# Attention of a hybrid encoder block: TensorE's order written out for all eight query blocks

## Chip, core and metric

The kernel runs on one core of a Trainium2 chip. The metric is the device time of one execution in microseconds, the median of three runs of the same program. TensorE's clock is 1.2 or 2.4 GHz, as granted; the profile gives it as a share of 2.4.

## What is computed

One layer on 1024 tokens of width 1024 in float32: a half-step feed-forward network (SwiGLU) with a layer norm, a mixer with a layer norm, and a second feed-forward network with a layer norm. Half of the mixer's width is a gated linear attention, the other half a sparse attention of 8 heads of width 64. Only the second matters here. For each query an indexer scores all admissible keys, and the best 256 are kept; then each head computes

```python
_, idx = lax.top_k(score, topk)
...
logits = jnp.einsum('bqhd,bqkhd->bqhk', qb, kg).astype(jnp.float32) * scale
logits = jnp.where(valid[:, :, None, :], logits, -jnp.inf)
p = jax.nn.softmax(logits, axis=-1)
return jnp.einsum('bqhk,bqkhd->bqhd', p.astype(vg.dtype), vg)
```

and the two halves, side by side, are multiplied by the output weights.

## The kernel before

The kernel gathers no keys. A mask of 0 and -1e30 per query and key (`bias`, which lies in the tiles of the scores) takes the place of the selection, and all keys up to the query block's end are used. The queries come in 8 blocks of 128 (b = 0 to 7); block b sees n = 128 (b + 1) keys. `attend_block` (L1043) does one block, in four pairs q of heads h = 2q + j:

- **Logits** (L1063, L1064): queries are the stationary operand, 128 x 128, keys the moving one, in chunks of 256 to 512 columns. Query and key are split into a high and a low part (`qq`, `ql`, and the key tiles named `xh` for even and `xl` for odd heads), so each chunk takes two matmuls into the PSUM tile `lg`, two of which exist.
- **Reduction** (L1067): VectorE adds the mask, writes `e` and the row's maximum `mx`; `nm` (L1078) is the scaled negative maximum. ScalarE makes the exponentials in place and their sum `sm` (L1079). Three `e` tiles take turns.
- **Transposes** (L1087): TensorE turns `e` in pieces of 128 x 128, up to four pieces to a PSUM tile `tpe` (a group); VectorE copies the even head's group to an SBUF tile `et` (L1092), ScalarE the odd head's (L1090). Blocks 4 to 7 have two groups a head. There are four `et` tiles. The PSUM tiles `tpe`, `rb` and `tp` share two banks.
- **Value products** (L1099): per block of keys and head, the values (128 keys x 64) are stationary, the transposed numerators the moving 128 columns. The even head writes partitions 0 to 63 of the PSUM tile `pv`, the odd head 64 to 127; so they use the array as 128 x 64 (`128*64` in the profile), while logits and transposes use it as 128 x 128.
- **End of a block**: VectorE copies `pv` to the right half of the tile `cat` (L1103); eight more 64-wide matmuls spread the reciprocals of the sums over `rb` (L1109), and VectorE multiplies (L1112).

Around it, `run` (L1452) loads the left half of `cat` by DMA, and for the first half of the tokens splits `cat` into high and low parts for the output projection (`split_cat`: transposes `tp` at L184), projects the previous block (`proj_tok`: `pt`, L654 to L656, 24 matmuls of 512 columns), adds to x1 and stores. `load_q` (L1030) brings the queries of the next block in four transfers, issued by SP.

No order is written out here. The program is built under a scheduler (`TileContext(nc, schedule_with_timeline_sim=True)`, L1578) that keeps data dependencies and buffer reuse, and otherwise orders each engine's instructions by its own estimate of times. `in_order` (L143) is the means against it: it chains all TensorE instructions made inside it in the order of the code. Before, it is used in the feed-forward parts only. Each engine executes its list strictly in order.

Of the kernel before, what the change touches and what calls it, by code (L numbers as in the profile page):

```python
# [18 lines left out]
P = 128  # L19
# [96 lines left out]
class Block:  # L116
    def __init__(self, ctx, tc, aps):
# [17 lines left out]
        self._ntile = 0  # L135
        self.fill = []
# [6 lines left out]
    def in_order(self, *engines):  # L143
# [7 lines left out]
        for i in body[start:]:  # L151
            if i.engine in (engines or (mybir.EngineType.PE,)):
# [7 lines left out]
                prev[i.engine] = i  # L160

# [881 lines left out]
    def attend_block(self, b, kst, vt, bias, q_dram, qp, ep, tp, rp, ps, cat):  # L1043
        nc = self.nc
        V = nc.vector
        n = (b + 1) * P
        w = n if n <= 512 else n // 2
        nch = n // w
        qq, ql = self.q_tiles[b]
        if b + 1 < NB and b + 1 not in self.q_tiles:  # L1050
            self.load_q(b + 1, q_dram, qp[(b + 1) % 2])
        po = self.ps_pj.tile([P, 4, P], F32, tag="pj", name=self.uid("pv"))
        sm = tp.tile([P, 8], F32, tag="sm", name=self.uid("sm"), bufs=2)
        for q in range(4):
            es = []
            for j in range(2):
                h = 2 * q + j
                k = kst[j][:, q, :]
                pl = ps.tile([P, 2, 512], F32, tag="lg", name=self.uid("lg"), bufs=2)
                for c in range(nch):  # L1060
                    out = pl[:, c, : max(w, 256)]
                    ks = slice(c * w, c * w + max(w, 256))
                    nc.tensor.matmul(out, qq[:, h, :], k[:, ks], start=True, stop=False)  # L1063
                    nc.tensor.matmul(out, ql[:, j, q, :], k[:, ks], start=False, stop=True)  # L1064
                e = ep[(2 * q + j) % 3].tile([P, T], F32, tag="e", name=self.uid("e"), bufs=1)
                mx = self.small.tile([P, 1], F32, tag="mx", name=self.uid("mx"))
                V.tensor_tensor_reduce(  # L1067
                    out=e[:, :n].rearrange("p (c w) -> p c w", c=nch),
                    in0=pl[:, :nch, :w],
                    in1=bias[b].rearrange("p (c w) -> p c w", c=nch),  # L1070
                    scale=1.0,
                    scalar=NEG,
                    op0=ALU.add,
                    op1=ALU.max,
                    accum_out=mx,
                )
                nm = self.small.tile([P, 1], F32, tag="nm", name=self.uid("nm"))
                V.tensor_scalar(nm, mx, -0.125, None, ALU.mult)  # L1078
                nc.scalar.activation(e[:, :n], e[:, :n], AF.Exp, bias=nm, scale=0.125, accum_out=sm[:, h : h + 1])  # L1079
                es.append(e)  # L1080
            for g in range(0, b + 1, 4):
                m = min(4, b + 1 - g)
                ets = []
                for j in range(2):
                    pt = self.ps_tp.tile([P, 4, P], F32, tag="tp", name=self.uid("tpe"))
                    for i in range(m):
                        nc.tensor.transpose(pt[:, i, :], es[j][:, (g + i) * P : (g + i + 1) * P], self.ident)  # L1087
                    et = tp.tile([P, 4, P], F32, tag="et", name=self.uid("et"), bufs=4)
                    if j:
                        nc.scalar.activation(et[:, :m, :], pt[:, :m, :], AF.Copy)  # L1090
                    else:
                        V.tensor_copy(et[:, :m, :], pt[:, :m, :])  # L1092
                    ets.append(et)
                for i in range(m):
                    kb = g + i
                    for j in range(2):
                        h = 2 * q + j
# [484 lines left out]
```

## Times and profile before

| what | value |
|---|---|
| median of 3 runs | 2049.46 us (2046.78 to 2050.31) |
| the profiled execution | 2050.26 us, its span 2048.5 us |
| TensorE matmuls | 1997.3 us busy (98%), mean granted clock 0.981 |
| VectorE, ScalarE, GpSimd | 72%, 40%, 28% busy |
| attention, first logits to last copy of `pv` | 1132.69 to 1314.10 us of the span |

Busy TensorE time is the union of records whose modelled ends overlap the next record, so a busy stretch can still hold slack: starts have to be compared with starts. A value product or a sum (the 64-wide work) leaves two records in the trace, every other matmul of the attention one.

### The profile page before, as it was taken

What the parts mean: (1) busy time and instruction counts of PE and PEld (TensorE: products, weight loads), DVE (VectorE), ACT (ScalarE), POOL (GpSimd) and SP (SyncE); (2) the same over time, 40 slices, a digit from 0 to 9 for tenths busy, and PEclk for the clock granted to TensorE, in tenths of its full rate; (3) what the DMA queues carried; (4) which work ended last, traced back from release to release, by engine and by line L of the source; (5) the groups of instructions that cost most, each with busy time, mean ns of one, the idle gap of its engine ahead of it and who ended that gap; (6) DMA issues with size and microseconds to landing.
All of it is one profiled execution on the core that took longest, in us unless ns stands there. A gap on an engine that the chain in (4) does not pass through costs nothing.

```text
span 2048.5 us, 26941 instructions
## 1 busy us (share of the span) xinstructions
PE 1997.3 (98%) x9752; PEld 1623.9 (79%) x9752; DVE 1474.6 (72%) x2326; ACT 824.5 (40%) x1320; POOL 581.1 (28%) x497
## 2 busy tenths in 40 slices
PE   8999999999999999998998999999999999999997
PEld 6888888888888788777876677787888888888886
DVE  5588788785668768899965455567687777766577
ACT  4332322324334445888253444334323323334341
POOL 3345444440001112144152000035354454420001
PEclk9999999999999999998997799999999999999999
DMA  5345445369656222022156430242354454487664
GB/s 174 114 144 186 144 154 185 134 230 322 195 177 205 89 93 83 11 63 73 32 140 160 121 80 17 89 169 73 124 183 147 143 181 154 146 279 272 201 194 150
DMA packets 192709, 298.44 MB, mean 146 GB/s; under 512 B 16304, under 2 KB 98368, under 8 KB 192576
## 3 DMA queue, kind: packets, MB, share of 16 engines
q1 hardware_dynamic: 192576, 296.72, 44.6%
q8 instruction: 77, 1.26, 0.2%
q14 instruction: 56, 0.46, 0.1%
HBM read 205.96 MB, written 90.70 MB: 145 GB/s over the span
## 4 chain that ended last, share of the span: by engine, by line
PE 87%; DVE 5%; ACT 3%; DMA 2%; issue 1%; POOL 1%; SPq 0%; POOLq 0%; DVEq 0%; ACTq 0%
PE pd L481 19%; PE pq L310 14%; PE pq L311 14%; PE pq L309 14%; PE pf L641 3%; PE pf L642 3%; PE pf L643 3%; PE pv L1099 3%; PE pt L654 2%; PE pt L655 2%; PE pt L656 2%; PE tpe L1087 2%; DVE junk L767 1%; PE tp L255 1%; PE lg L1063 1%
## 5 line engine op out<-in xcount | busy, mean ns | idle before, releaser
L97 DVE TENSOR_TENSOR wloq<-rw,whiq 128x512 fp32r<-128x512 f32 (+1 forms) x208 | 211.9, 1021 | 111.4 <-ACT whiq L96 110.8
L97 DVE TENSOR_TENSOR wlod<-rd,whid 128x1024 fp32r<-128x1024 f32 x154 | 186.2, 1219 | 130.4 <-ACT whid L96 129.6
L96 ACT ACTIVATE whid<-rd 128x1024 fp32r<-128x1024 f32 x154 | 160.9, 1059 | 244.7 <-PE pd L481 173.1
L96 ACT ACTIVATE whiq<-rw 128x512 fp32r<-128x512 f32 (+1 forms) x208 | 163.5, 806 | 224.1 <-POOL rw L295 94.2
L481 PE MATMUL pd<-wlod,whid 128*128 128x512 f32 x616 | 239.7, 389 | 0.8 <-DVE wlod L97 0.8
L481 PE MATMUL pd<-whid,wlod 128*128 128x512 f32 x616 | 239.3, 389 | 0.0
L481 PE MATMUL pd<-whid 128*128 128x512 f32 x616 | 234.9, 391 | 0.7 <-ACT whid L96 0.7
L309 PE MATMUL pq<-b_h,whiq 128*128 128x512 f32 x576 | 228.9, 398 | 2.2 <-ACT b_h L96 2.2
L310 PE MATMUL pq<-b_l,whiq 128*128 128x512 f32 x576 | 225.4, 391 | 0.9 <-DVE b_l L97 0.9
L311 PE MATMUL pq<-b_h,wloq 128*128 128x512 f32 x576 | 225.1, 391 | 0.0
L197 POOL TENSOR_TENSOR rs<-ve,neghalf 128x1 f32<-128x1 f32 x24 | 33.8, 1410 | 630.5 <-DVE ve L215 630.5
L421 ACT ACTIVATE c<-c 128x512 f32<-128x512 f32 x80 | 50.4, 632 | 238.2 <-DVE c L345 146.6
L309 PE MATMUL pq<-xh,whiq 128*128 128x512 f32 x352 | 137.7, 391 | 0.0
L311 PE MATMUL pq<-xh,wloq 128*128 128x512 f32 x352 | 137.0, 389 | 0.0
L310 PE MATMUL pq<-xl,whiq 128*128 128x512 f32 x352 | 136.9, 389 | 0.0
L481 PEld LDWEIGHTS pd<-wlod,whid 128*128 128x128 f32 x616 | 115.6, 188 | 25.4 <-DVE wlod L97 1.6
L481 PEld LDWEIGHTS pd<-whid 128*128 128x128 f32 x616 | 115.6, 188 | 25.0 <-ACT whid L96 1.3
L481 PEld LDWEIGHTS pd<-whid,wlod 128*128 128x128 f32 x616 | 115.6, 188 | 24.0
L654 PE MATMUL pt<-whi,xh 128*128 128x512 f32 x320 | 128.3, 402 | 5.3 <-ACT stage L1397 3.3
L309 PEld LDWEIGHTS pq<-b_h,whiq 128*128 128x128 f32 x576 | 108.7, 189 | 23.9 <-ACT b_h L96 2.8
L655 PE MATMUL pt<-wlo,xh 128*128 128x512 f32 x320 | 127.0, 398 | 0.1
L311 PEld LDWEIGHTS pq<-b_h,wloq 128*128 128x128 f32 x576 | 108.7, 189 | 23.2
(253 smaller groups left out, 4538.5 us busy)
## 6 DMA issues: line engine op xcount, KB each, us to landing
rw<-in_ffn_w_gu_dram SPq DMA_DIRECT2D x88, 512.0 KB, 4.2
rd<-h_dram SPq DMA_DIRECT2D x154, 256.0 KB, 3.4
h_dram<-c SPq DMA_DIRECT2D x148, 256.0 KB, 3.0
rt<-in_ffn_w_down_dram SPq DMA_DIRECT2D x44, 512.0 KB, 3.4
t_dram<-rt SPq DMA_DIRECT2D x44, 512.0 KB, 2.9
rd<-t_dram SPq DMA_DIRECT2D x88, 256.0 KB, 4.0
rd<-in_ffn_w_down_dram SPq DMA_DIRECT2D x66, 256.0 KB, 4.0
raw<-in_w_in_dram SPq DMA_DIRECT2D x20, 512.0 KB, 4.0
```

Source lines behind the costliest of these rows:

```text
L96: self.nc.scalar.activation(hi, src, AF.Copy)
L97: self.nc.vector.tensor_sub(lo, src, hi)
L309: mm(bank, wh[:, k, :], xh[:, k, :], start=(start and k == 0), stop=False)
L310: mm(bank, wh[:, k, :], xl[:, k, :], start=False, stop=False)
L311: mm(bank, wl[:, k, :], xh[:, k, :], start=False, stop=(stop and k == 3))
L481: nc.tensor.matmul(bank, left, right, start=(i == 0 and n == 0), stop=(i == ng - 1 and n == 2))
L641: nc.tensor.matmul(pt[:m], wh[:, k, :m], xh[:, k, :], start=(k == 0), stop=False)
L642: nc.tensor.matmul(pt[:m], wh[:, k, :m], xl[:, k, :], start=False, stop=False)
L643: nc.tensor.matmul(pt[:m], wl[:, k, :m], xh[:, k, :], start=False, stop=(k == KD - 1))
L654: nc.tensor.matmul(pt, xh[:, k, cols], wh[:, k % 2, :], start=(k == 0), stop=False)
L655: nc.tensor.matmul(pt, xh[:, k, cols], wl[:, k % 2, :], start=False, stop=False)
L1099: nc.tensor.matmul(po[j * 64 : j * 64 + 64, q, :], v, ets[j][:, i, :], start=(kb == 0), stop=(kb == b))
```

## The change

The loop over blocks and pairs becomes one sequence over all 64 heads, numbered x = 8b + h, and 32 pairs p. `attend` takes the place of `attend_block`, with `begin(b)` and `end(b)` for what `run` did around it. Four inner functions hold the old steps: `logits(x)`, `turned(x)` (transposes and copies), `values(p)` (the value products of both heads of a pair over all their blocks of keys, heads alternating) and `divided(b)`. TensorE's order is chained by `in_order`: three heads' logits first, then per pair the transposes of the even head, the logits of head 2p + 3, the transposes of the odd head, the logits of head 2p + 4, and the products. The work of `end` is made inside `any_order`, which leaves it out of the chain, so the scheduler still places it. Two details change with it: `e` tiles turn by x instead of the head's number in the block, and the engine that copies a group alternates by head and group, not by head alone.

```diff
@@ in_order @@
-            if i.engine in (engines or (mybir.EngineType.PE,)):
+            if i.engine in (engines or (mybir.EngineType.PE,)) and i.name not in self.loose:
+    @contextmanager
+    def any_order(self):
+        last = self.nc.cur_bb.bb.instructions[-1]
+        yield
+        body = self.nc.cur_bb.bb.instructions
+        start = next(k for k in reversed(range(len(body))) if body[k] is last) + 1
+        self.loose.update(i.name for i in body[start:])
@@ attend_block, now attend @@
-    def attend_block(self, b, kst, vt, bias, q_dram, qp, ep, tp, rp, ps, cat):
+    def attend(self, kst, vt, bias, q_dram, qp, ep, tp, rp, ps, begin, end):
-        for q in range(4):
-            es = []
-            for j in range(2):
-                h = 2 * q + j
...
-                e = ep[(2 * q + j) % 3].tile([P, T], F32, tag="e", name=self.uid("e"), bufs=1)
...
-            for g in range(0, b + 1, 4):
-                m = min(4, b + 1 - g)
-                ets = []
-                for j in range(2):
-                    pt = self.ps_tp.tile([P, 4, P], F32, tag="tp", name=self.uid("tpe"))
-                    for i in range(m):
-                        nc.tensor.transpose(pt[:, i, :], es[j][:, (g + i) * P : (g + i + 1) * P], self.ident)
...
-                    if j:
-                        nc.scalar.activation(et[:, :m, :], pt[:, :m, :], AF.Copy)
-                    else:
-                        V.tensor_copy(et[:, :m, :], pt[:, :m, :])
-                    ets.append(et)
-                for i in range(m):
-                    kb = g + i
-                    for j in range(2):
...
+        def logits(x):
+            b, h = divmod(x, 8)
...
+            e = ep[x % 3].tile([P, T], F32, tag="e", name=self.uid("e"), bufs=1)
...
+        def turned(x):
...
+            for g in range(0, b + 1, 4):
...
+                if (x + g // 4) % 2:
+                    nc.scalar.activation(et[:, :m, :], pt[:, :m, :], AF.Copy)
+                else:
+                    V.tensor_copy(et[:, :m, :], pt[:, :m, :])
+                ets[x].append(et)
+        def values(p):
...
+            et = [ets.pop(2 * p + j) for j in range(2)]
+            for kb in range(b + 1):
                 for j in range(2):
+                    h = 2 * q + j
+                    nc.tensor.matmul(
+                        out[b][j * 64 : j * 64 + 64, q, :],
+                        vt[kb // 4][:, kb % 4, h * 64 : (h + 1) * 64],
+                        et[j][kb // 4][:, kb % 4, :],
+                        start=(kb == 0),
+                        stop=(kb == b),
+                    )
+        def divided(b, cat):
...
+        with self.in_order():
+            for x in range(3):
+                logits(x)
+            for p in range(4 * NB):
+                b, q = divmod(p, 4)
+                if q == 0:
+                    cat = begin(b)
+                    if b + 1 < NB and b + 1 not in self.q_tiles:
+                        self.load_q(b + 1, q_dram, qp[(b + 1) % 2])
+                turned(2 * p)
+                logits(2 * p + 3)
+                turned(2 * p + 1)
+                logits(2 * p + 4)
+                values(p)
+                if q == 3:
+                    divided(b, cat)
+                    with self.any_order():
+                        end(b, cat)
@@ run @@
-                for b in range(NB):
+                def begin(b):
...
-                    self.attend_block(b, kst, vt, bias, q_dram, qp, ep, tp, rp, ps, c)
+                    return c
+                def end(b, c):
                     if b < 4:
                         self.split_cat(c, b, [[c0[0]], [c0[1]]])
...
+                self.attend(kst, vt, bias, q_dram, qp, ep, tp, rp, ps, begin, end)
```

Outside the attention both programs list the same instructions in the same order on all engines. Inside, TensorE's lists read as follows; line numbers of the changed program differ: L1075 and L1076 are the logits, L1102 the transposes, L1118 the products, L1134 the sums, L1512 and L1510 the store and load of x1's half, L1047 and L1048 those of the queries.

TensorE at the last pair of block 4, before (the stretch that rows 3 show):

```order
L1087 MATMUL tpe_10579<-ident,e_10562 128x128 x4
L1099 MATMUL pv_10393<-et_10553,vt_9597 64x128
L1063 MATMUL lg_10671<-xl_9579,qq_9588 128x384
L1064 MATMUL lg_10671<-xl_9579,ql_9589 128x384
L1063 MATMUL lg_10671<-xl_9579,qq_9588 128x384
L1064 MATMUL lg_10671<-xl_9579,ql_9589 128x384
L1087 MATMUL tpe_10586<-ident,e_10573 128x128 x4
L1099 MATMUL pv_10393<-et_10584,vt_9596 64x128
L1087 MATMUL tpe_10601<-ident,e_10562 128x128
L1099 MATMUL pv_10393<-et_10591,vt_9596 64x128
L1099 MATMUL pv_10393<-et_10584,vt_9596 64x128
L1099 MATMUL pv_10393<-et_10591,vt_9596 64x128
```

and the same pair in the change, from the transposes of its odd head on:

```order
L1102 MATMUL tpe_10613<-ident,e_10552 128x128 x4
L1102 MATMUL tpe_10620<-ident,e_10552 128x128
L1075 MATMUL lg_10624<-xh_9578,qq_9588 128x384
L1076 MATMUL lg_10624<-xh_9578,ql_9589 128x384
L1075 MATMUL lg_10624<-xh_9578,qq_9588 128x384
L1076 MATMUL lg_10624<-xh_9578,ql_9589 128x384
L1118 MATMUL pv_10471<-et_10596,vt_9596 64x128
L1118 MATMUL pv_10471<-et_10618,vt_9596 64x128
L1118 MATMUL pv_10471<-et_10596,vt_9596 64x128
L1118 MATMUL pv_10471<-et_10618,vt_9596 64x128
L1118 MATMUL pv_10471<-et_10596,vt_9596 64x128
L1118 MATMUL pv_10471<-et_10618,vt_9596 64x128
```

A first product no longer stands alone between transposes: both heads' transposes and the next logits come first, and ten products follow each other, of which six are shown.

TensorE at the end of block 6, before (`pv` of one number is block 6, `rb` its sums):

```order
L1099 MATMUL pv_10911<-et_11147,vt_9597 64x128
L1109 MATMUL rb_11164<-ident,rc_11162 64x128 x8
L1063 MATMUL lg_11244<-xh_9578,qq_9588 128x512
L1064 MATMUL lg_11244<-xh_9578,ql_9589 128x512
L1063 MATMUL lg_11244<-xh_9578,qq_9588 128x512
L1064 MATMUL lg_11244<-xh_9578,ql_9589 128x512
L1099 MATMUL pv_10911<-et_11153,vt_9597 64x128
L1099 MATMUL pv_10911<-et_11147,vt_9597 64x128
L1099 MATMUL pv_10911<-et_11153,vt_9597 64x128
L1099 MATMUL pv_10911<-et_11147,vt_9597 64x128
L1099 MATMUL pv_10911<-et_11153,vt_9597 64x128
L1063 MATMUL lg_11255<-xl_9579,qq_9588 128x512
```

and in the change:

```order
L1118 MATMUL pv_10993<-et_11144,vt_9597 64x128
L1118 MATMUL pv_10993<-et_11168,vt_9597 64x128
L1134 MATMUL rb_11198<-ident,rc_11196 64x128 x8
L1102 MATMUL tpe_11210<-ident,e_11113 128x128 x4
L1102 MATMUL tpe_11217<-ident,e_11113 128x128 x4
L1075 MATMUL lg_11224<-xl_9579,qq_9588 128x512
L1076 MATMUL lg_11224<-xl_9579,ql_9589 128x512
L1075 MATMUL lg_11224<-xl_9579,qq_9588 128x512
L1076 MATMUL lg_11224<-xl_9579,ql_9589 128x512
L1102 MATMUL tpe_11235<-ident,e_11151 128x128 x4
L1102 MATMUL tpe_11242<-ident,e_11151 128x128 x4
L1075 MATMUL lg_11249<-xh_9578,qq_9588 128x512
```

Where the next logits and the rest of the products followed the sums, the transposes of the next block's first head now follow them, and logits only after these.

SP's queue in blocks 1 and 2, before (`x_dram<-score` is the store of x1's half, `score<-x_dram` the next load, `qq` and `ql` the queries of block 3):

```order
L1455 DMA cat_10387<-og_dram 128x512
L1038 DMA ql_9589<-q_lo_82 64x4x128
L1037 DMA qq_9588<-q_hi_81 64x8x128 x2
L1467 DMA x_dram<-score_6535 128x512
L1038 DMA ql_9589<-q_lo_82 64x4x128
L1464 DMA score_6535<-x_dram 128x512
L1455 DMA cat_10652<-og_dram 128x512
```

and in the change:

```order
L1499 DMA cat_10421<-og_dram 128x512
L1048 DMA ql_9589<-q_lo_82 64x4x128
L1047 DMA qq_9588<-q_hi_81 64x8x128
L1513 DMA x_dram<-score_6535 128x512
L1047 DMA qq_9588<-q_hi_81 64x8x128
L1048 DMA ql_9589<-q_lo_82 64x4x128
L1510 DMA score_6535<-x_dram 128x512
L1499 DMA cat_10686<-og_dram 128x512
```

The store of x1 has moved ahead of the second half of a query load.

## Rows read from the trace of the kernel before

**Rows 1.** The page of the profiled execution: the span, part 1 (busy time of each engine, share of the span, instructions) and part 4 (the chain that ended last, by engine).

```profile
span 2048.5 us, 26941 instructions
...
PE 1997.3 (98%) x9752; PEld 1623.9 (79%) x9752; DVE 1474.6 (72%) x2326; ACT 824.5 (40%) x1320; POOL 581.1 (28%) x497
...
PE 87%; DVE 5%; ACT 3%; DMA 2%; issue 1%; POOL 1%; SPq 0%; POOLq 0%; DVEq 0%; ACTq 0%
```

**Rows 2.** Busy time by stretches, one row for each query block 0 to 7. The first stretch begins with the first logits, each ends where the copy L1103 of its block starts. Columns: length, then busy us and instructions of TensorE, its weight loads, VectorE, ScalarE and GpSimd, the granted TensorE clock as a share of 2.4 GHz, the busy share of the DMA engines, GB/s.

```profile
1132.69:1148.61 15.92, 15.29 (x64) 10.39 (x64) 7.03 (x43) 7.29 (x32) 2.04 (x3) 0.53 0.70 186
1148.61:1166.10 17.49, 16.40 (x109) 11.89 (x110) 9.26 (x37) 7.57 (x23) 0.00 (x0) 1.00 0.59 136
1166.10:1185.59 19.49, 19.07 (x133) 13.95 (x134) 10.54 (x33) 8.30 (x22) 0.00 (x0) 1.00 0.33 83
1185.59:1208.16 22.57, 22.25 (x167) 17.25 (x168) 12.77 (x36) 10.33 (x23) 0.00 (x0) 1.00 0.29 82
1208.16:1236.77 28.61, 27.59 (x197) 20.48 (x198) 14.73 (x38) 11.54 (x26) 0.00 (x0) 1.00 0.18 47
1236.77:1261.20 24.43, 24.12 (x191) 17.43 (x192) 14.11 (x34) 11.88 (x24) 0.00 (x0) 1.00 0.16 34
1261.20:1288.47 27.27, 26.38 (x217) 19.33 (x216) 15.73 (x36) 13.00 (x23) 0.00 (x0) 1.00 0.00 1
1288.47:1314.10 25.63, 24.23 (x229) 18.56 (x228) 14.94 (x32) 13.66 (x25) 0.00 (x0) 1.00 0.06 16
```

**Rows 3.** Timeline of TensorE alone at the end of block 4. Columns: start (us), time from the first start to the last modelled end, line, operation, output<-inputs, tile of the array, shape, records merged (a value product leaves two records, a transpose or a logits matmul one).

```profile
1228.05 1.09 PE L1099 MATMUL pv<-et,vt 128*64 128x128 f32 x16
1229.08 0.66 PE L1087 MATMUL tpe<-ident,e 128*128 128x128 f32 x4
1229.66 0.43 PE L1099 MATMUL pv<-et,vt 128*64 128x128 f32 x2
...
1230.83 0.60 PE L1087 MATMUL tpe<-ident,e 128*128 128x128 f32 x4
1231.36 0.43 PE L1099 MATMUL pv<-et,vt 128*64 128x128 f32 x2
1231.72 0.33 PE L1087 MATMUL tpe<-ident,e 128*128 128x128 f32 x1
1232.18 1.09 PE L1099 MATMUL pv<-et,vt 128*64 128x128 f32 x14
1233.19 0.33 PE L1087 MATMUL tpe<-ident,e 128*128 128x128 f32 x1
```

**Rows 4.** Timeline of SP's DMA issues, from block 0 to the start of block 2 (columns as above; the time is that of issuing).

```profile
1139.64 0.63 SPq L1038 DMA_DIRECT2D ql<-q_lo  x1
...
1141.02 0.92 SPq L1455 DMA_DIRECT2D cat<-og_dram  x2
...
1157.81 0.58 SPq L1038 DMA_DIRECT2D ql<-q_lo  x1
...
1162.29 0.57 SPq L1038 DMA_DIRECT2D ql<-q_lo  x1
```

**Rows 5.** DMA issues with their time to landing, issues between 1139.5 and 1140.2 us. Columns: output<-input, queue, count, size, median us from issue to landing.

```profile
ql<-q_lo SPq DMA_DIRECT2D x1, 128.0 KB, 4.8
```

**Rows 6.** The same view, issues between 1141.0 and 1141.5 us.

```profile
cat<-og_dram SPq DMA_DIRECT2D x1, 256.0 KB, 7.7
```

**Rows 7.** Timeline of TensorE alone around the first logits of block 1 and the end of block 0.

```profile
1143.35 0.69 PE L1099 MATMUL pv<-et,vt 128*64 128x128 f32 x2
1143.97 0.58 PE L1063 MATMUL lg<-xh,qq 128*128 128x256 f32 x1
...
1149.08 0.60 PE L184 MATMUL tp<-ident,cat 128*128 128x128 f32 x4
```

**Rows 8.** Timeline of VectorE alone at the end of block 5.

```profile
1261.20 0.69 DVE L1103 COPY cat<-pv 128x512 f32<-128x512 f32 x1
1261.81 0.14 DVE L1078 TENSOR_SCALAR nm<-mx 128x1 f32<-128x1 f32 x1
...
1262.83 0.68 DVE L1112 TENSOR_TENSOR cat<-cat,rb 128x512 f32<-128x512 f32 x1
```

**Rows 9.** Groups of instructions of the whole attention (1132.6 to 1316 us), shapes kept apart. Columns: line, engine, operation, output<-inputs, shapes, count | busy us, mean ns of one | idle time of the engine just before, and what ended it.

```profile
L1099 PE MATMUL pv<-et,vt 128*64 128x128 f32 x576 | 61.9, 287 | 2.2 <-ACT et L1090 1.5 <-DVE et L1092 0.4
...
L1099 PEld LDWEIGHTS pv<-et,vt 128*64 128x64 f32 x576 | 39.4, 138 | 22.0 <-issue 10.3 <-ACT et L1090 4.4 <-ACT e L1079 2.5
...
L1067 DVE CUSTOM_DVE_ANT_0 e<-lg,score 128x1024 f32<-128x1024 f32 x8 | 9.6, 1218 | 1.2 <-PE lg L1064 0.9 <-PE tpe L1087 0.3
...
L1078 DVE TENSOR_SCALAR nm<-mx 128x1 f32<-128x1 f32 x64 | 9.3, 150 | 0.9
L1079 ACT ACTIVATE e<-e,nm 128x1024 f32<-128x1024 f32 x8 | 9.1, 1144 | 3.2 <-DVE nm L1078 3.2
```

**Rows 10.** What TensorE's matmuls waited for in the attention (1132 to 1316 us): who waited <- for whom: us in total, times, longest.

```profile
PE tpe L1087 <- DVE et L1092: 2.0, 4, 0.8
PE pv L1099 <- ACT et L1090: 1.5, 4, 0.4
PE tpe L1087 <- DVE cat L1112: 1.1, 3, 0.5
```

More of the change, by code (lines that the diff above doesn't have):

```diff
@@ L135, in __init__ @@
         self._ntile = 0
+        self.loose = set()
         self.fill = []
@@ L1081, in attend_block @@
+        def turned(x):
+            b = x // 8
+            e = es.pop(x)
+            ets[x] = []
             for g in range(0, b + 1, 4):
                 m = min(4, b + 1 - g)
[L1083 to L1093 removed]
@@ L1094, in attend_block @@
-                for i in range(m):
-                    kb = g + i
-                    for j in range(2):
-                        h = 2 * q + j
-                        v = vt[kb // 4][:, kb % 4, h * 64 : (h + 1) * 64]
-                        nc.tensor.matmul(
-                            po[j * 64 : j * 64 + 64, q, :], v, ets[j][:, i, :], start=(kb == 0), stop=(kb == b)
-                        )
-        dsa = cat[:, 512:].rearrange("p (k t) -> p k t", k=4)
-        V.tensor_copy(dsa, po)
@@ L1104, in attend_block @@
-        rc = rp.tile([P, 8], F32, tag="rc", name=self.uid("rc"), bufs=2)
-        V.reciprocal(rc, sm)
-        rb = self.ps_tp.tile([P, 4, P], F32, tag="tp", name=self.uid("rb"))
-        for h in range(8):
-            rows = slice(h % 2 * 64, h % 2 * 64 + 64)
-            nc.tensor.matmul(
-                rb[rows, h // 2, :], rc[:, h : h + 1].to_broadcast([P, 64]), self.ident, start=True, stop=True
-            )
-        V.tensor_mul(dsa, dsa, rb)
+                pt = self.ps_tp.tile([P, 4, P], F32, tag="tp", name=self.uid("tpe"))
@@ new lines, in turned @@
+                for i in range(m):
+                    nc.tensor.transpose(pt[:, i, :], e[:, (g + i) * P : (g + i + 1) * P], self.ident)
+                et = tp.tile([P, 4, P], F32, tag="et", name=self.uid("et"), bufs=4)
+                if (x + g // 4) % 2:
[6 more added lines that the diff above has]
+            if q == 0:
+                out[b] = self.ps_pj.tile([P, 4, P], F32, tag="pj", name=self.uid("pv"))
+            et = [ets.pop(2 * p + j) for j in range(2)]
+            for kb in range(b + 1):
+                for j in range(2):
+                    h = 2 * q + j
[5 more added lines that the diff above has]
+                        stop=(kb == b),
+                    )
@@ new lines, in divided @@
+        def divided(b, cat):
+            dsa = cat[:, 512:].rearrange("p (k t) -> p k t", k=4)
+            V.tensor_copy(dsa, out.pop(b))
+            rc = rp.tile([P, 8], F32, tag="rc", name=self.uid("rc"), bufs=2)
+            V.reciprocal(rc, sums.pop(b))
+            rb = self.ps_tp.tile([P, 4, P], F32, tag="tp", name=self.uid("rb"))
+            for h in range(8):
+                rows = slice(h % 2 * 64, h % 2 * 64 + 64)
+                nc.tensor.matmul(
+                    rb[rows, h // 2, :], rc[:, h : h + 1].to_broadcast([P, 64]), self.ident, start=True, stop=True
+                )
+            V.tensor_mul(dsa, dsa, rb)
```

63 lines of the change are left out of this document (33 added, 30 removed).

## Prediction

> **What bounds the kernel now.** I read the page first: over the program TensorE is busy 98% of the span, and the chain that ended last lies on it for 87% [rows 1]. So a change pays by what TensorE's own sequence loses, not by what another engine saves. Both programs list the same instructions in the same order on every engine outside the attention, so I then cut the trace at the eight copies L1103 that end the query blocks. In each block TensorE is busy all but 0.3 to 1.4 us, VectorE only 44 to 58% of the time [rows 2]. Blocks 1 to 7 run at 2.4 GHz; block 0 runs almost wholly at 1.2 GHz (mean grant 0.53), while the DMA engines are 0.70 busy.
>
> "Busy" hides the loss, because each record (0.29 us for half a value product [rows 9]) overlaps its neighbours. So I read from start to start, on TensorE's timeline [rows 3]. A value product takes 1231.72 - 1231.36 = **0.36 us** alone, between transposes; in a run, eight take 1229.08 - 1228.05 = **1.03 us** and seven take 1233.19 - 1232.18 = 1.01 us. In a run the products of a pair's two heads overlap two by two, and the place of a missing partner is paid for. Alone a product fills two places, so a place costs (1.02 - 0.36) / 6 = 0.11 us, and each run pays 0.14 us once. The neighbours pay too. A transpose streams 128 columns as half a product does; at 0.11 us each, four need 0.44. Up to a product, four that follow logits take 1231.36 - 1230.83 = 0.53 us, four that also follow a product 1229.66 - 1229.08 = 0.58 us. So the turn to products costs 0.09 to 0.12, the turn back 0.05. Together a run of 64-wide work (products and the sums rb, L1109) costs **0.31 us, and 0.11 us for each place** (its instructions, rounded up to an even number).
>
> **The change, part by part.**
>
> *Products in one run.* Counted in the two orders, from the first logits to the end of the attention: 89 runs now, 82 of odd length, 434 places for 352 instructions; in the change 37 runs, 10 odd, 362 places. The order shows why: now a pair's first product stands alone, then come a transpose and the others. Saved are 52 x 0.31 + 72 x 0.11 = 16.1 + 7.9 = **24.0 us**; by block, 0 to 7: 1.6, 1.1, 1.6, 1.6, 4.4, 5.5, 4.9, 3.4. The late blocks, with two groups of keys, have the most runs now.
>
> *Block 0 gives nothing.* SP's queue does not move there. The last transfer of block 1's queries is issued at 1139.64 [rows 4] and lands 4.8 us later [rows 5], at 1144.4. The first logits of block 1, which start at 1143.97 now [rows 7], are pinned in the change ahead of block 0's last two pairs of products: three lone products at 1143.97 - 1143.35 = 0.6 us each and a transpose less lie before them, so TensorE is there at about 1142 and waits some 2.4 us, with everything behind it. The first `cat` is issued at 1141.02 [rows 4] and lands 7.7 us later [rows 6], at 1148.7; the transposes that read it (1149.08 now, [rows 7]) follow block 0, as before. So block 0 still ends near 1148.6, and I strike out its 1.6: **-22.4 us**.
>
> *The end of a block.* In the change the sums and then the next block's transposes follow at once, where now logits lie between. The second PSUM tile of transposes after the sums needs their bank, free after VectorE's copy and multiplication: from the last product 0.3 us to its end, 0.61 to the next start on VectorE, 0.68, and two handovers of 0.05 [rows 8], 1.7 us. TensorE has 0.9 us of sums and 0.44 of transposes to do meanwhile; 0.4 is left, taken as 0.5, at seven boundaries: **+3.5 us**. Bounds: 0, and 1.7 each or 12 us, if a reduction of 1.22 us [rows 9] is in VectorE's way every time. I take the low value because VectorE is idle over 40% of each of these blocks [rows 2].
>
> *Waits that go.* TensorE waits 2.0 + 1.5 us for copies of transposed numerators now and 1.1 us for that bank [rows 10]. With the next logits between the last transposes and the products, I let 3.5 of these 4.6 go; bounds 0 and 4.6. The two terms cancel: **0**, bounds -4.6 and +12.
>
> *Logits ahead.* Between a head's logits and its transposes now lie two other heads' logits, a run of products and a transpose group; in block 7, with 16 places, over 4 us. Reduction, scaling and exponential need 1.22 + 0.15 + 1.14 = 2.5 us [rows 9]. Nothing is late. That `e` tiles turn by the running number makes each three heads old also over a block's end; hidden by the same margin, nothing.
>
> *At nothing.* The copies of groups alternate otherwise, but stay 48 on ScalarE and 48 on VectorE. On SP a store of x1 moves ahead of half a query load in three blocks; the load has a whole block (17 us or more) until its logits, and its issues take 1157.81 to 1162.29 now [rows 4]. If that cover were gone, see rival 3.
>
> Sum: 2050.26 - 22.4 = 2027.9 us for the profiled execution. The median of the three runs is 0.8 lower: the forecast is **2027 us**.
>
> One rule of the Trainium skill speaks against the largest term: "TensorE: Matmul & The Clock Gate", under "The mechanism" in Part 3, lets weight loads run beside matmuls only where their row groups differ, and both heads' products use all rows. By that rule it would be rival 4, 2034. The rows disagree: eight products hold 16 loads of 138 ns [rows 9], 2.2 us, within their 1.03 us [rows 3].
>
> **Rivals.**
> 1. *Copies become the bound.* If at half of the 28 pairs of blocks 1 to 7 the products wait 1 us for a copy behind a reduction on VectorE, that is +14: 2041. For it: VectorE works in order, with reductions of up to 1.22 us [rows 9]. Against: it has 14.9 us to do in a block 7 that shrinks from 25.6 to 22.2 [rows 2]. By the skill's "TensorEngine Tiling (Array Packing)", PSUM Bottleneck, packing products leaves the copies out of PSUM as they were and may make them the bound; these busy shares say not yet.
> 2. *The clock stays low.* The wait of 2.4 us lies in the stretch at 1.2 GHz. Were block 1 at 1.2 GHz too, its 16.4 us of TensorE work [rows 2], part of it waiting, would grow by up to 8: 2035. Against: the order of block 0 now, with its lone products, is no denser, and the grant rose.
> 3. *Slower: pinned logits wait for their queries.* Nothing may pass them, so a late load stops TensorE once in each of blocks 1 to 6. The load is released about one block ahead; this decides only where its last piece lands over 10 us later than now. To eat 22.4 us, six loads must be 3.7 us later still; at 5 us past that point each: 2027 + 30 = 2057. Against: from block 2 on DMA is a third busy or less [rows 2].
> 4. *Two heads' products do not overlap*: the 66 places saved in blocks 1 to 7, 66 x 0.11 = 7.3 us, are not earned: 2034. Against: rows 3.
> 5. *A turn costs nothing; its gap is a wait that moves along*: then only those 7.3 us are earned: 2042. Against: the gaps at both sides of products are alike to 0.03 us wherever they stand [rows 3]; waits would vary.
>
> **How the numbers follow.** Forecast 0.80; rivals 1: 0.07, 2: 0.06, 3: 0.02, 4: 0.02, 5: 0.03. The range begins where block 0's 1.6 and all the waits are gained as well, 2027 - 1.6 - 4.6, about 2021. It ends at 2037, past rivals 2 and 4, and with the block ends at most of their upper bound; rivals 1, 3 and 5 are left out. A measurement can tell 0.2%, 4 us, from no change. Faster by more: the forecast and rivals 1, 2, 4 and most of 5, 0.95; within it: 0.03; slower: 0.02.
>
> **What would show it.** In the trace after, the copies out of `pv` should lie about 18.9 us apart for block 5 (24.4 now), 22.3 for block 6 (27.3), and the first should start 16 us after the first logits, as now. Products should stand in runs, 0.14 + 0.11 us for each place; TensorE should wait some 0.5 us for the multiplication after the sums at seven block ends, and before the first logits of block 1. The forecast is wrong if a place in a long run costs more than 0.13 us, if transposes and products wait more than 10 us in sum for copies, or if block 0 changes by more than 3 us. The stretch after the attention should keep its length.

## The result and the profile after

The changed kernel takes 2028.88 us (median; 2027.62 to 2034.01), the kernel before 2049.28 us on the same chip: a ratio of 0.9903, 95% interval 0.9891 to 0.9914. Two later measurements, each with the kernel before on the same chip beside it, gave 0.9898 [0.9883, 0.9913] and 0.9902 [0.9887, 0.9916]. The forecast was 2027 us.

The page of the profiled execution (its own time 2034.01 us, the longest of the four), answering to [rows 1]:

```profile
span 2032.2 us, 26938 instructions
...
PE 1978.1 (97%) x9752; PEld 1618.8 (80%) x9752; DVE 1477.5 (73%) x2326; ACT 825.3 (41%) x1320; POOL 580.9 (29%) x497
...
PE 77%; DVE 8%; DMA 5%; issue 4%; ACT 3%; POOL 2%; SPq 0%; POOLq 0%; DVEq 0%; ACTq 0%
```

TensorE is still busy nearly all of the span, with 19 us less to be busy for. That its share of the chain that ended last is 77% here, after 87% before, belongs to this execution: two later profiles of the same program have 82% and 87%. Now the same stretches as in [rows 2], query blocks 0 to 7, with the same columns (the copy that ends each is L1128 now):

```profile
1134.34:1148.05 13.71, 10.08 (x51) 7.34 (x52) 7.17 (x43) 6.88 (x31) 2.04 (x3) 0.62 0.62 164
1148.05:1169.69 21.64, 19.62 (x114) 14.29 (x112) 9.73 (x35) 8.11 (x24) 0.00 (x0) 0.80 0.60 126
1169.69:1188.38 18.69, 18.05 (x136) 13.54 (x134) 10.97 (x35) 7.90 (x22) 0.00 (x0) 1.00 0.44 112
1188.38:1209.07 20.69, 20.40 (x166) 16.24 (x164) 12.66 (x35) 10.68 (x25) 0.00 (x0) 1.00 0.33 85
1209.07:1233.03 23.96, 23.20 (x201) 19.24 (x198) 14.74 (x38) 11.83 (x27) 0.00 (x0) 1.00 0.24 56
1233.03:1252.09 19.06, 18.86 (x196) 16.20 (x194) 14.42 (x35) 12.16 (x25) 0.00 (x0) 1.00 0.20 43
1252.09:1273.72 21.63, 21.42 (x220) 18.34 (x218) 15.86 (x35) 13.64 (x25) 0.00 (x0) 1.00 0.00 1
1273.72:1297.91 24.19, 22.04 (x234) 18.42 (x232) 15.04 (x30) 13.30 (x23) 0.00 (x0) 1.00 0.01 2
```

Read the clock column first: block 1 has a mean grant of 0.80 and takes 21.64 us. In a second profile of the same program (below, the run e9_changed_again) it is granted 0.99 and takes 17.50 us, and blocks 2 to 7 agree within 0.05 us. So those 4.1 us belong to this execution; the program's steps are judged by the other, of which blocks 0, 1 and 7 are:

```profile
1132.80:1147.35 14.55, 11.20 (x51) 8.06 (x52) 7.22 (x43) 6.88 (x31) 2.04 (x3) 0.50 0.66 174
1147.35:1164.85 17.50, 16.01 (x114) 11.78 (x112) 9.55 (x36) 8.01 (x24) 0.00 (x0) 0.99 0.57 138
...
1268.86:1293.05 24.19, 22.04 (x234) 18.42 (x232) 15.03 (x29) 13.30 (x23) 0.00 (x0) 1.00 0.01 2
```

From the first logits to the last copy out of `pv` it takes 160.25 us there, against 181.41 before: 21.2 us less, where the forecast had 22.4. What lies behind keeps its length (span less the end of the last stretch: 734.4 us before, 734.3 and 734.5 now, 735.4 in a third profile, e1_again's; about 1 us of it varies from one execution to the next).

TensorE's timeline in blocks 4 and 5 (columns as in [rows 3]) shows the products in whole runs:

```profile
1231.65 1.31 PE L1118 MATMUL pv<-et,vt 128*64 128x128 f32 x20
1232.79 1.04 PE L1134 MATMUL rb<-ident,rc 128*64 128x128 f32 x16
1233.76 0.66 PE L1102 MATMUL tpe<-ident,e 128*128 128x128 f32 x4
1234.62 0.44 PE L1102 MATMUL tpe<-ident,e 128*128 128x128 f32 x2 [0.20 <-DVE cat L1137]
...
1240.99 0.34 PE L1075 MATMUL lg<-xh,qq 128*128 128x384 f32 x1
1241.16 0.34 PE L1076 MATMUL lg<-xh,ql 128*128 128x384 f32 x1
1241.43 1.53 PE L1118 MATMUL pv<-et,vt 128*64 128x128 f32 x24
1242.89 0.87 PE L1102 MATMUL tpe<-ident,e 128*128 128x128 f32 x6
```

Twelve products (24 records) take 1242.89 - 1241.43 = 1.46 us; by the forecast's prices 0.14 + 12 x 0.11 = 1.46. The turn from logits shows ahead of them: 0.27 us from the last logits' start, where logits follow logits after 0.17. At the block's end four transposes need 0.44 us of 1234.62 - 1233.76 = 0.86; the gap of 0.42 is the wait for the multiplication of the sums (the row itself shows 0.20 of it, since it counts from the modelled end of the transposes before).

What TensorE's matmuls waited for in the attention, answering to [rows 10] (this and the next views are of the first profile):

```profile
PE lg L1075 <- DMA qq<-q_hi: 1.8, 1, 1.8
PE tp L194 <- DMA cat<-og_dram: 1.6, 1, 1.6
PE pv L1118 <- DVE nm L1090: 1.3, 1, 1.3
PE lg L1075 <- DVE mx L1079: 1.2, 1, 1.2
PE tpe L1102 <- DVE cat L1137: 1.2, 6, 0.2
PE tpe L1102 <- DVE xl L196: 0.9, 2, 0.6
PE tpe L1102 <- DVE et L1107: 0.8, 2, 0.4
```

The waits before were small and spread out; now single ones stand out, in blocks 0, 1 and 7. TensorE at the turn of blocks 0 and 1 (compare [rows 7]):

```profile
1143.26 0.27 PE L1102 MATMUL tpe<-ident,e 128*128 128x128 f32 x1
1145.30 0.36 PE L1075 MATMUL lg<-xh,qq 128*128 128x256 f32 x1 [1.77 <-DMA qq<-q_hi]
...
1147.76 1.92 PE L1134 MATMUL rb<-ident,rc 128*64 128x128 f32 x16
1151.29 0.63 PE L194 MATMUL tp<-ident,cat 128*128 128x128 f32 x4 [1.61 <-DMA cat<-og_dram]
```

And block 7, TensorE and then VectorE, at the third pair:

```profile
1289.45 1.31 PE L1118 MATMUL pv<-et,vt 128*64 128x128 f32 x18
1292.05 1.09 PE L1118 MATMUL pv<-et,vt 128*64 128x128 f32 x14 [1.29 <-DVE nm L1090]
```

```profile
1289.50 1.89 DVE L204 TENSOR_TENSOR xl<-cat,xh 128x512 fp32r<-128x512 f32 x3
1291.31 0.68 DVE L1107 COPY et<-tpe 128x512 f32<-128x512 f32 x1
```

The products stop after nine of sixteen. The releaser given is an early VectorE instruction; the one that the remaining products read is the copy behind it, which ends at 1291.99. Ahead of the copy stand three subtractions L204 (the low halves of earlier blocks' `cat`, which only the projection after the attention reads).

### The profile page after: what moved, and what is told of

It reads as the page before. It is cut to its first block, busy times and chain, and to the rows that moved or that the text cites. A ratio compares the mean times of both kernels' runs of the same rounds, so it can differ in the third digit from the quotient of the medians.

```text
span 2032.2 us, 26938 instructions
## 1 busy us (share of the span) xinstructions
PE 1978.1 (97%) x9752; PEld 1618.8 (80%) x9752; DVE 1477.5 (73%) x2326; ACT 825.3 (41%) x1320; POOL 580.9 (29%) x497
## 3 DMA queue, kind: packets, MB, share of 16 engines
q8 instruction: 76, 1.25, 0.3%
## 4 chain that ended last, share of the span: by engine, by line
PE 77%; DVE 8%; DMA 5%; issue 4%; ACT 3%; POOL 2%; SPq 0%; POOLq 0%; DVEq 0%; ACTq 0%
PE pd L491 18%; PE pq L320 12%; PE pq L319 12%; PE pq L321 12%; PE pf L651 3%; PE pf L652 3%; PE pf L653 3%; DVE junk L777 2%; PE pv L1118 2%; PE pt L664 2%; PE tpe L1102 2%; PE pt L666 1%; PE pt L665 1%; PE tp L265 1%; DMA rd<-in_ffn_w_down_dram 1%
## 5 line engine op out<-in xcount | busy, mean ns | idle before, releaser
L491 PEld LDWEIGHTS pd<-whid,wlod 128*128 128x128 f32 x616 | 115.6, 188 | 24.2
```

The lines of the kernel that those rows point to most:

```text
L491: nc.tensor.matmul(bank, left, right, start=(i == 0 and n == 0), stop=(i == ng - 1 and n == 2))
```

## The experiments

All kernels are edits of the changed kernel. Where a time is compared with that of the changed kernel, the blocks of the profiles stand beside it, since they repeat far better than the total.

**The changed kernel again, twice.**

> The changed kernel once more, unaltered. If the fall of the clock in block 1 of the first profile (1.2 GHz from about 1154 to 1160 us) belongs to the program, each profile shows one there, block 1 takes 21 us and more, and the median stays at 2029 within 2. If it is chance, the clock stays at 2.4 GHz through block 1, which then takes 17 to 18.5 us, and the profiled run is 3 to 5 us under the first one's 2034.

> The changed kernel once more, as the measure on the same chip for the two runs beside it. Expected 2028 to 2032 us, the attention's blocks as in its earlier profiles (18.7, 20.7, 24.0, 19.1, 21.6 and 24.2 us for blocks 2 to 7), block 1 at 17.6 us, or at 21.6 us if the granted clock falls to 1.2 GHz in it again.

Measured: 2031.18 us (before beside it: 2050.07) and 2030.77 (before: 2050.36). Blocks 1 to 7 took 17.59, 18.68, 20.69, 23.96, 19.05, 21.62, 24.23 us and 17.50, 18.64, 20.74, 23.96, 19.06, 21.61, 24.19. The slow block 1 appears in one profile of three. The profiled execution of e1_again is 1.6 us under the first one's 2034.01, not 3 to 5: its attention is 3.1 us shorter, but it starts 0.4 us later and the stretch behind it is 1.1 us longer.

**Without the fixed order** (the scheduler again chooses TensorE's order; logits ahead and joined products as written):

```diff
-        with self.in_order():
+        with ExitStack():
```

> The changed code without its chain: the scheduler places TensorE's instructions again. In its order there are 72 runs of 64-wide work with 414 places (before 89 and 434, changed 37 and 362). Theory (0.31 us a run, 0.11 us a place): 7.4 us less than before and 16.6 us more than the changed kernel, so 2042 to 2046. Rival (what counts is that the code has the logits one and a half pairs ahead, not the runs): within 5 us of the changed kernel, 2029 to 2034.

Measured: 2040.65 us (ratio to before 0.9953 [0.9940, 0.9965]), 9.5 above the changed kernel: between the two ranges, 1.4 us short of the theory's 2042 and far above the rival's. The order that came out has 72 runs with 414 places, against 37 and 362: by the prices 16.6 us more. The attention is 12.3 us longer than in e1_again (172.73 against 160.48); a free order moves other work into some of the waits (5.8 us of them in its trace, 9.0 in e9_changed_again's), and with these 3.2 us the 12.3 are 15.5 of the 16.6. So about half of the gain hangs on the fixed order; the other half is still there when the scheduler orders the new code.

**The runs cut in three by logits, places unchanged** (`logit_steps(x)` is `logits(x)`, halting at two places in its second half of keys):

```diff
-        def values(p):
+        def values(p, rest):
...
             for kb in range(b + 1):
+                if kb in ((b + 1) // 3, 2 * (b + 1) // 3):
+                    next(rest, None)
...
-                logits(2 * p + 4)
-                values(p)
+                rest = logit_steps(2 * p + 4)
+                next(rest, None)
+                values(p, rest)
```

> The changed kernel, but in the 16 pairs followed by logits of two chunks each run of products is parted in three by the second chunk's two matmuls, which stood ahead of the run. The same instructions, 69 runs in place of 37, places as before at 362, no instruction moved by more than one run. Theory (a turn costs): 32 x 0.31 = 9.9 us, and 0.05 more per turn back to logits, 11.5; a few us of waits for copies may come on top, since less lies ahead of the products: +10 to +15, 2039 to 2044. Rival (the gaps at a turn are waits that move along): +0 to +4.

Measured: 2045.60 us (0.9978 [0.9968, 0.9988]), 14.4 above the changed kernel (the attention is 16.5 longer), for 69 runs and 362 places. Rival 5 of the prediction, that a turn costs nothing, falls: it allows next to none of that. TensorE's timeline in its block 5, where the twelve products of a pair stand in three runs:

```profile
1243.67 1.13 PE L1128 MATMUL pv<-et,vt 128*64 128x128 f32 x8
1244.72 0.45 PE L1081 MATMUL lg<-xh,qq 128*128 128x384 f32 x1
1245.10 0.66 PE L1128 MATMUL pv<-et,vt 128*64 128x128 f32 x8
1245.69 0.44 PE L1084 MATMUL lg<-xh,ql 128*128 128x384 f32 x1
1246.06 0.66 PE L1128 MATMUL pv<-et,vt 128*64 128x128 f32 x8
```

Four products take 1245.69 - 1245.10 = 0.59 us = 0.14 + 4 x 0.11, and a logits matmul between them 0.37 instead of 0.17: an extra run costs 0.14 + 0.20 = 0.34 us where the prediction had 0.31 between transposes; 32 of them make 10.9. The first run of a pair takes 1.05 here, 0.47 more: with half a head's logits less ahead of it, it waits for its copies (ScalarE's ends at 1244.09; behind the first product, TensorE goes on at 1244.14). In block 5, longer by 23.69 - 19.05 = 4.6 us, eight runs make 2.7 and the four first runs 1.5.

That a turn costs something agrees with the Trainium skill, "TensorEngine Tiling (Array Packing)", Tiling Modes: a change of the tiling mode drains the engine. The page gives no figure for it; in these rows it is 0.34 us for going to the products and back.

**The two heads' products one after the other**, in the same run:

```diff
-            for kb in range(b + 1):
-                for j in range(2):
+            for j in range(2):
+                for kb in range(b + 1):
```

> The changed kernel with the products of a pair in the order of heads: all of the even head, then all of the odd one, still one run. 37 runs as in the changed kernel. Theory (products of the two heads overlap two by two, and a place without partner is paid for): 288 products fill 288 places more, less the few that stood alone, at 0.11 us: +28 to +32 us, 2057 to 2061, slower than before. Rival (they do not overlap; a run is cheap because its weight loads are hidden in any order): +0 to +3 us.

Measured: 2048.64 us (0.9988 [0.9979, 0.9996]), 17.5 above the changed kernel: without the alternation nearly all of its gain of 18.9 us is lost, so two heads do overlap, and rival 4 falls. This is not a share of the gain: the kernel before had the overlap too, wherever its products stood two by two, and the change itself saves 72 places, 7.9 us by the forecast. My 28 to 32 was too much. One run of ten products in block 4, and a run of ten in the same block of the first profile:

```profile
1223.86 2.02 PE L1118 MATMUL pv<-et,vt 128*64 128x128 f32 x20
1225.81 0.77 PE L1102 MATMUL tpe<-ident,e 128*128 128x128 f32 x5
```

```profile
1227.54 1.31 PE L1118 MATMUL pv<-et,vt 128*64 128x128 f32 x20
1228.79 0.77 PE L1102 MATMUL tpe<-ident,e 128*128 128x128 f32 x5
```

Head after head it takes 1.95 us, alternating 1.25 (by the forecast's prices 0.14 + 10 x 0.11 = 1.24); with no overlap, two places for each product, it would be 2.34. Its single records explain the middle: seven start 0.11 us apart from 1223.86 (the first two 0.16); from 1224.57 records start 0.05 us apart, until 1224.95; then 0.11 again. The odd head starts before the even one is through. What the Trainium skill states under "TensorEngine Tiling (Array Packing)", Tiling Modes, fits this: tiles of the array run independently of one another. The other rule of the Trainium skill, weighed in the prediction ("TensorE: Matmul & The Clock Gate", Part 3), would have let this order cost nothing; it cost 17.5 us.

**No logits ahead**, order and joined products kept:

```diff
-            for x in range(3):
-                logits(x)
...
+                logits(2 * p)
+                logits(2 * p + 1)
                 turned(2 * p)
-                logits(2 * p + 3)
                 turned(2 * p + 1)
-                logits(2 * p + 4)
                 values(p)
```

> The changed kernel with its fixed order kept, but with no logits ahead: in each pair of heads TensorE does the pair's two logits, then both heads' transposes, then the pair's products. What it tells apart: whether the gain needs the logits ahead, or only the order and the joined products. My theory: with nothing to do between a head's logits and its transposes, TensorE waits in each pair for the maximum, the exponentials and the scaling of the same pair; a replay of the changed kernel's durations in this order gives an attention some 77 us longer than the changed kernel's 163.6 us, so about 2105 us (2090 to 2120), slower than before (about 2050), with most of TensorE's waits in the attention put down to ScalarE's exponentials or VectorE's maximum. Rival (the order alone makes the gain, since VectorE and ScalarE are fast enough between two halves of a pair): 2029 to 2040 us.

Measured: 2146.82 us (1.0462 [1.0446, 1.0478]), 116 above the changed kernel. TensorE's timeline at one pair, and three of its blocks (1, 4 and 5, cut within 0.3 us of the copies that end them; columns as in [rows 2]):

```profile
1295.04 0.34 PE L1076 MATMUL lg<-xl,ql 128*128 128x384 f32 x1
1297.74 0.88 PE L1102 MATMUL tpe<-ident,e 128*128 128x128 f32 x6 [2.37 <-ACT e L1091]
```

```profile
1151.00:1178.70 27.70, 22.25 (x114) 15.50 (x112) 9.31 (x35) 7.02 (x22) 0.00 (x0) 0.75 0.37 80
...
1245.00:1283.60 38.60, 28.33 (x202) 21.88 (x198) 14.43 (x39) 11.59 (x26) 0.00 (x0) 0.91 0.15 35
1283.60:1323.70 40.10, 28.22 (x195) 23.46 (x193) 14.15 (x36) 11.71 (x24) 0.00 (x0) 0.79 0.10 20
```

The sign and the mechanism were right: the wait for the pair's own exponentials, 2.37 us in this pair. The size was not. The expectation left out the clock: blocks 1 to 7, in which TensorE now stands in every pair, have mean grants of 0.75 to 0.91, where the changed kernel has 1.00 in blocks 2 to 7. Of the 117 us by which the attention is longer than in e9_changed_again, 64 are idle time of TensorE (72.8 us against 9.1) and 53 are more busy time of the same matmuls (204.6 against 151.2). Of the two orders tried, the pinned one pays with the logits ahead and loses without them.

**At a block's start the logits ahead come before the transposes:**

```diff
-                turned(2 * p)
-                logits(2 * p + 3)
+                if q == 0 and b > 0:
+                    logits(2 * p + 3)
+                    turned(2 * p)
+                else:
+                    turned(2 * p)
+                    logits(2 * p + 3)
```

> The changed kernel with one step moved: at the first pair of each block from block 1 on, the logits ahead come before the transposes of the even head, so that TensorE has logits to do between the block's sums and the next transposes. It takes away the wait at a block's end, which the trace of the changed kernel shows as 1.2 us over 6 transposes that wait for VectorE's scaling of the sums, and 2.6 us in all before the weight loads of the same stretches. My theory (the wait is about 0.5 us in each of 6 or 7 blocks, and the move costs no run of products, but a turn between logits and transposes may cost 0.1 to 0.3): 0 to 3 us faster than the changed kernel, most likely 1 to 2, about 2028 us. Rival (what waits at the block's end is the transfer or the turn itself, and the wait only moves behind the logits): no difference, or up to 2 us slower.

Measured: 2030.72 us (0.9900 [0.9884, 0.9917]); the attention 160.75 us, against 160.25 and 160.48 in the two undisturbed profiles of the changed kernel. The waits for the multiplication are gone from its list, but those of transposes for VectorE's copies grew from 1.5 us (in e9_changed_again) to

```profile
PE tpe L1102 <- DVE et L1107: 3.1, 4, 1.7
```

The rival was right: the wait only moves.

**The two small edits undone:**

```diff
-            e = ep[x % 3].tile([P, T], F32, tag="e", name=self.uid("e"), bufs=1)
+            e = ep[x % 8 % 3].tile([P, T], F32, tag="e", name=self.uid("e"), bufs=1)
...
-                if (x + g // 4) % 2:
+                if x % 2:
```

> The changed kernel with its two small edits undone: the tile of the exponentials is chosen by the head's number in its block modulo 3 again (so that around a block's end two heads in three share a tile one head too early), and the copies of the transposes go to ScalarE or VectorE by head and no longer by half head in turn. My prediction took both at nothing. Theory: 0 to 3 us slower than the changed kernel, 2029 to 2033 us (a replay of the durations gives 2.1). Rival (with the order pinned, a pair's copies on one engine come late, and each of 32 pairs waits some 0.3 us): 8 to 12 us slower, about 2040 us.

Measured: 2031.89 us (0.9907 [0.9892, 0.9921]), not told apart from the changed kernel in the time; the attention 161.88 us, 1.6 longer: as the theory had it, and the rival falls. Blocks 4 to 6 take 25.30, 20.15 and 22.51 us, 3.3 more in sum, and block 7 22.38, 1.8 less. "Nothing" was right for the sum alone: together the two small edits help in three blocks and cost in the last. There the three subtractions L204 stand on VectorE in this run too, from 1289.27, but the third pair's copies on VectorE are through before them, at 1288.05. Which of the two edits does what in blocks 4 to 6 was not separated.

**The end of block 0 behind block 1's second pair:**

```diff
-                    with self.any_order():
-                        end(b, cat)
+                    if b == 0:
+                        cat0 = cat
+                    else:
+                        with self.any_order():
+                            end(b, cat)
+                if p == 5:
+                    end(0, cat0)
```

> The changed kernel with the end of block 0 (the transposes of its attention output, which wait for a transfer that lands late in block 1) put behind block 1's second pair of heads, at a fixed place. In the trace of the changed kernel TensorE stood 1.6 us for that transfer in block 1, and in one of its two profiled executions the granted clock fell to 1.2 GHz behind the wait, and block 1 took 21.64 us where it took 17.59 in the other. Theory: the wait goes, block 1 takes 15.5 to 17 us, and the time is 1 to 3 us shorter than the changed kernel, about 2027 to 2029 us; the low clock in block 1 comes no more, or as seldom as before. Rival (TensorE stands for the queries and for the first exponentials of the block anyway, so the 1.6 us only turn up at the next wait): no difference (within 1 us), with block 1 at 17.5 us or longer.

Measured: 2029.25 us (0.9892 [0.9877, 0.9906]), no difference that can be told; its block 1:

```profile
1147.36:1164.84 17.48, 16.58 (x115) 12.26 (x113) 9.31 (x35) 8.61 (x26) 0.00 (x0) 0.98 0.85 144
```

17.48 us, as in the two other profiles of the changed kernel. The wait for the transfer is gone and the block is no shorter: the theory falls. What took the place of the wait was not followed further.

**The subtractions of blocks 0 to 6 on GpSimd** (three of the seven run in block 7), and that together with the edit above:

```diff
-        self.nc.vector.tensor_sub(xl, dsa, xh)
+        sub = self.nc.vector if b == NB - 1 else self.nc.gpsimd
+        sub.tensor_sub(xl, dsa, xh)
```

> The changed kernel with one kind of instruction moved to another engine: the subtraction that makes the low half of the attention's second output, for blocks 0 to 6, runs on GpSimd, which does next to nothing in the attention, and no longer on VectorE. In the changed kernel's trace three of these (1.89 us together) stand on VectorE in block 7 ahead of the copy of a transpose, and TensorE's products of the third pair pause 1.29 us for it; my prediction had block 7 at 22.2 us and it took 24.2 us. Theory (VectorE's queue makes the pause): the pause goes, block 7 takes 22.3 to 23 us and the others what they took, so the time is 1.2 to 1.9 us shorter than the changed kernel beside it. Rival (TensorE's third pair would then wait for the exponentials and ScalarE's copies, which end at the same time, or GpSimd's subtractions, some 1.5 us each, come late for the projection): block 7 at 24 us or the stretch behind the attention over 1 us longer, and no difference in the time.

> The subtractions on GpSimd and the end of block 0 behind block 1's second pair, together. Theory: the two act in different blocks and add: 1 to 3 us shorter than the changed kernel beside it, nearly all of it from block 7. Rival: nothing of either is seen in the time, within 1 us.

Measured: 2028.38 us (0.9889 [0.9874, 0.9904]) and 2028.61 (0.9889 [0.9872, 0.9905]), beside 2030.77 for the changed kernel on the same chip. Block 7 of the first, by stretch, on TensorE and on GpSimd:

```profile
1270.91:1293.41 22.50, 21.64 (x234) 18.23 (x232) 13.29 (x27) 13.23 (x23) 3.75 (x3) 1.00 0.01 2
```

```profile
1286.61 1.97 PE L1119 MATMUL pv<-et,vt 128*64 128x128 f32 x32
1288.51 1.09 PE L1103 MATMUL tpe<-ident,e 128*128 128x128 f32 x8
```

```profile
1285.50 3.75 POOL L205 TENSOR_TENSOR xl<-cat,xh 128x512 fp32r<-128x512 f32 x3 [75.37 <-ACT e L1092]
```

The sixteen products run through in 1.90 us = 0.14 + 16 x 0.11, and block 7 takes 22.50 us, 1.7 less than in the three profiles of the changed kernel; blocks 2 to 6 stay within 0.1 us, and the stretch behind the attention does not grow (734.6 us). The cause of 1.7 of the 2.0 us of block 7's excess is shown. That the whole kernel is faster for it (2.4 us by the medians) is likely, but the intervals overlap. The second edit adds nothing here either.

## Why the prediction was right

By its own steps:

- **Products in one run, 24.0 us.** The price of a place is confirmed to 0.01 us by runs of 10, 12 and 16 places (1.24 to 1.25, 1.46, 1.90 us), the overlap by e4_heads_apart. That a run has a price is shown by e3_runs_in_three, with 0.34 us between logits. The 0.31 of the forecast, between transposes, was not isolated: the rows it names give 0.14 + 0.09 + 0.05 = 0.28, and its 0.12 for the turn to products is in none of them; with 0.28 the term is 22.5. Blocks 2 to 7 were counted at 17.9, 21.0, 24.2, 18.9, 22.4 and 22.2 us and take 18.6, 20.7, 24.0, 19.1, 21.6 and 24.2 in the second profile: blocks 3 to 5 within 0.3, blocks 2, 6 and 7 not. Block 2 has 0.7 us of waits, as much as its excess: 0.4 for the multiplication at its start and 0.3 for VectorE's `xl`.
- **Block 0 gives nothing.** Right in substance, wrong in the mark I set: the first copy starts 14.55 us after the first logits and not 16, but the sums (1.9 us in the view above) now run mostly behind that boundary and are paid in block 1. Blocks 0 and 1 together were forecast at 15.9 + 16.4 = 32.3 us and take 32.05 in the second profile. The wait for the queries is there: 1.77 us, 1.5 in the second profile, where I had 2.4. "Nothing is late" did not hold in block 0: ahead of that wait TensorE stands 1.2 us for a maximum and 0.7 us for exponentials, where it stood 0.4 and 0.2 before.
- **The end of a block, +3.5.** Six ends at 0.42 make 2.5 us. The seventh boundary, behind block 0, waits for the transfer of `cat` instead.
- **Waits that go, -3.5.** This is the term that was mis-sized. Transposes and products waited 2.0 + 1.5 us for copies before [rows 10], and 0.4 us more that no row there shows; in the second profile it is 1.5 and 0.2 us of transposes and 1.3 us of products, 3.0 in all, so 0.9 went. The 1.1 us for the bank is part of the 2.5 us of the block ends now. Block 6 lost its wait of before:

```profile
PE pv L1099 <- ACT et L1090: 0.8, 2, 0.4
```

  It took 21.6 us against a forecast of 22.4. But block 7 took 24.2 against 22.2: there a copy did wait, behind 1.9 us of work that the attention does not need, and the products with it for 1.29 us; a transpose waited 0.4 us. The margin of "over 4 us" counted reduction, scaling and exponential, and left out what else the scheduler may put on VectorE between them. It is rival 1 in one pair, not in fourteen. e10_subtractions_on_gpsimd removes it and finds 1.7 of the 2.0 us.
- **The sum.** -22.4 forecast, -21.2 in the attention of the second profile, -20.9 in e1_again's, -23.3 with the subtractions moved. With 2.5 for the ends and 0.9 + 1.1 for the waits the forecast's own sum would be -21.9; with 0.28 for a run as well, -20.4. The medians of the three measurements lie 18.9 to 20.4 us below those of before. How near they come to the 2027 is in part luck: they differ by 2.3 us among themselves, and the stretches ahead of and behind the attention, which the change leaves alone, vary by 1 to 2 us (the first logits start at 1132.80, 1134.34 and 1134.77 us in the three profiles). What is confirmed is the attention. None of the three signs of being wrong came: a place costs 0.11 us, the waits for copies are 3.0 us, and block 0 is 1.4 us shorter (2.2 in the first profile).
- **Rival 2** (the clock stays low in block 1) came true in part in the first profile, and not in the two others: 4.1 us, where I had allowed 8. **Rivals 4 and 5** fell to e4_heads_apart and e3_runs_in_three. **Rival 3** did not come true: SP's queue and the later queries delay nothing (the list of waits has one wait for queries, in block 0).

## What to carry to other kernels

Count an engine's turns, not only its instructions: here a run of half-width products costs 0.3 us on top of its places, and a lone product takes the 0.22 us of two, which no busy share shows, and starts on the timeline do. Fix an engine's order together with what it waits for: with the logits issued one and a half pairs ahead the fixed order gained 19 us, with none ahead it was 116 us slower than that; nothing between was tried. When one engine's order is pinned, look at the queues of the others for work that is not urgent: three subtractions at a bad place cost 1.7 us.

## What the runs showed of the hardware

- **The granted clock can fall in one execution of a program and not in the next.** In the first profile TensorE stood 1.77 us at 1143.5 and 1.61 us at 1149.7, and block 1 was granted 0.80 in the mean, part of it at the 1.2 GHz level:

```profile
1154.00:1160.00 6.00, 6.00 (x20) 4.38 (x20) 1.14 (x5) 1.42 (x6) 0.00 (x0) 0.50 0.59 134
```

  The second profile has the same order with waits of 1.5 and 0.4 us there, then 1.1 us for a copy, and a grant of 0.99 in block 1. In block 0 it was the other way round: 0.62 in the first profile and 0.50 in the second. The difference is 4.1 us, more than most single edits here are worth, so a step of that size should be read from a block that repeats.
- **Two heads overlap even when they are issued one after the other**, in part: ten products took 1.95 us, between 1.25 in alternation and the 2.34 that no overlap would take.
- **GpSimd takes 1.25 us for the subtraction that VectorE does in 0.63** (3.75 and 1.89 us for three), and in this stretch that costs nothing that the times show: GpSimd has no other work in block 7 (0.00 us busy in the changed kernel).
